# Where the reciprocal square roots of all row norms are computed: eight VectorE instructions, or two or three on GpSimd

## The chip, the cores and the metric

The kernel runs on one core of a Trainium2 chip. The metric is the device time of one execution in microseconds (us). A core has five engines that run their own instruction streams and wait for each other through semaphores: TensorE (PE in the profile, with PEld for its weight loads), VectorE (DVE), ScalarE (ACT), GpSimd (POOL) and SyncE (SP, which issues the DMAs here).

## The reference, cut to what matters

Two layers of an encoder work on 768 tokens of 1024 features (512 of one request group, "S", and 256 of another, "P"). Layer 0 mixes tokens with a chunked gated unit, layer 1 with long convolutions; both add cross-attention to 256 memory tokens and a gated feed-forward part. Every sub-layer is normalised before and after:

```python
def rms_norm(x, g):
    y = xf * lax.rsqrt(jnp.mean(xf * xf, axis=-1, keepdims=True) + NORM_EPS)
    return y * g
def layer_norm(x, g, b):
    return (xf - mu) * lax.rsqrt(var + LN_EPS) * g + b
...
    hn = rms_norm(x, p['norm_mix_pre'][i])
    ... out = jnp.concatenate([mix, att], axis=-1) @ p['w_out'][i]
    x = x + rms_norm(out, p['norm_mix_post'][i])
    hn = rms_norm(x, p['norm_ffn_pre'][i])
    f = conv_ffn(hn, ...)
    x = x + rms_norm(f, p['norm_ffn_post'][i])
```

## The kernel before, in words

Tokens are handled in six row tiles of 128 (t = 0 to 3 are S, 4 and 5 are P). Every float32 operand of a large product is split into two parts ("hi" and "lo"), and a product is three matmuls; ACT writes hi, DVE writes lo (`split`). Rows become feature-major operands (`hT`, tiles hTS and hTP) by eight transposes on PE for each row tile (tiles `tps`), split by ACT and DVE.

`rstd_of` turns one column of 128 sums of squares into 128 reciprocal square roots. It is called 62 times: 24 times in `pre_norm` (tile names rstd, rstdm, rstdq: six at the start, and six behind the first output projection, the first down projection and the second output projection), 24 times in `out_proj`'s `half1` (rpost: six in each of four projections, which here are called out0, down0, out1 and down1), 8 times in `kv` (mr) and 6 times in `norm_v` (lnr). Behind a projection one row tile passes through this chain: the last matmul of its bank (rp), ACT's Square with a sum, rpost, two DVE instructions that add the residual (xr), for all but the last projection ACT's Square of the new x, rstd, DVE's scaling (y, or hn at the start), eight transposes on PE, the split. At the end of the program the two xr halves go out by DMA.

The order in which an engine takes its instructions is not written by hand. `Order` records what the kernel states and then runs a list schedule: each engine takes, among the instructions that it takes for ready, the one of the lowest rank; rank is the place in the stated order plus an offset from the table BIAS, and readiness comes from the durations in `cost` and the delays in LAT. So the numbers in `cost`, and the count of instructions stated ahead, set the order on all engines. Engines run their streams in that order. The attention's score matmuls (tiles `sc`) use 64 of the 128 rows of the array, two heads on the two halves; the other large products use 128 rows.

Of the kernel before, what the change touches and what calls it, by code (L numbers as in the profile page):

```python
# [30 lines left out]
# Buffers that the kinds of tiles may hold at once.  # L31
ROLES = {'xr': ('x', 3), 'y': ('y', 4), 'x0': ('x', 3), 'mem': ('mem', 2), 'mn': ('mem', 2), 'praw': ('pr', 2), 'hn': ('y', 4)}
T4, WR, WS, M8, M4 = 7, 2, 4, 14, 13
# How far in stated order the schedule may run ahead of its oldest instruction left, and by how many places the
# instructions of a part of the kernel (by kind) stand later than stated when an engine chooses.
# [52 lines left out]
def rstd_constants(n):  # L88
    """Newton's step and the third-order step on r multiply its limit by factors of their own; so the estimate aims
    at -(z / m) ** 0.5, the first step at (a / m) ** 0.5 and the second at (n / m) ** 0.5."""  # L90
    k1 = (3.0 * math.sqrt(n) / 8.0) ** 0.2
    k0 = (k1 / 2.0) ** (1.0 / 3.0)
    return k0 * k0, k1 * k1, float(0x5F3759DF + math.log2(k0) * 2 ** 23 - 2 ** 31)

class Order:
    """Takes down instructions as the kernel states them and hands them to Tile in the order of a list schedule:
    whenever an engine is free it takes the first stated instruction whose operands and buffers are there."""  # L100
# [17 lines left out]
    @contextmanager  # L118
    def of(self, part=None, load=None):
        """What is stated inside belongs to this part of the kernel; loads are the weights' way in."""  # L120
        keep = self.part, self.load
        self.part, self.load = part or self.part, self.load if load is None else load
        yield
        self.part, self.load = keep
# [8 lines left out]
    def tile(self, pool, shape, dt, tag, bufs, name, kind=None, cap=0):  # L133
        """A tile takes one of its tag's buffers, and one of the cap that its kind may hold."""
        t = pool.tile(list(shape), dt, tag=tag, name=name, bufs=bufs)
        self.tiles[t.tensor.name] = dict(res=[(tag, bufs)] + ([(kind, cap)] if kind else []), ops=[])
        return t

# [60 lines left out]
    @staticmethod  # L199
    def cost(eng, method, kw, args, outs, ins):  # L200
        n = max(int(np.prod([c for s, c in x.ap[1:]])) for x in outs)
        psum = any(x.space == bass.MemoryType.PSUM for x in ins)
        if eng == "tensor":
            if method == "transpose":
                return 110
            if kw["rhs"].dtype == F32R:
                return n / 2.4 if n >= 256 else 229
            return 20 + 4 * n / 2.4
        if eng == "scalar":
            c = (52 if psum else 95) + 0.833 * n  # L210
            return c + (190 if isinstance(kw.get("bias"), bass.AP) or isinstance(kw.get("scale"), bass.AP) else 0) + \
                (90 if "accum_out" in kw else 0)
        if eng == "vector":
            if method in ("tensor_scalar", "tensor_copy") and not psum:
                return 68 + 0.522 * n
            if method == "tensor_reduce" or method == "bn_stats":
                n = max(int(np.prod([c for s, c in x.ap[1:]])) for x in ins)
            return (130 if method == "scalar_tensor_tensor" else 69) + 1.042 * n
        if eng == "gpsimd":
            return 148 + 2.105 * n  # L220
        return 450

# [1 line left out]
    def schedule(self):  # L224
# [42 lines left out]
        def allowed(i):  # L267
            """Buffers for the tiles that start at i; the instructions before it must still fit in stated order."""
            at = ready_t[i]
            for name in first.get(i, ()):  # L270
                for tag, b in self.tiles[name]["res"]:
                    j = pos[name, tag]
                    if not free[tag]:
                        return None
                    at = max(at, min(free[tag]))
                    s, k = seq[tag], nxt[tag]
                    while k < len(s) and s[k][0] < oldest:
                        k += 1
                    nxt[tag] = k
                    if k < j:  # L280
                        later = sum(1 for x in ahead[tag] if x >= k)
                        live = sum(1 for x in s[max(0, k - 4 * b):k] if left[x[2]])
                        if live + later + 1 > b:
                            return None
                        for q in range(k, j):
                            if q in ahead[tag]:
                                later -= 1
                            elif left[s[q][2]] and serial[tag][q] + later + 1 > b:
                                return None
            return at  # L290
# [90 lines left out]
class FM:  # L381
    """Feature-major hi/lo pair: k-tiles of 128 features, S tokens and P tokens in tiles of their own."""
# [29 lines left out]
class Pairs:  # L412
    """Feature-major hi/lo pair in tiles of two k-tiles each."""
# [18 lines left out]
class Prog:  # L432
# [47 lines left out]
    def presplit(self):  # L480
        """Layer 1's mixer weights split while the matrix products of layer 0's feed-forward part hold the time."""
# [28 lines left out]
    def rstd_of(self, ss, n, eps, name, add=None):  # L510
        """(ss / n + eps) ** -0.5 (ss + add for ss when there is one), from an estimate out of the exponent bits by
        one step of second and one of third order; the steps' factors are folded into the estimate."""
        v = self.nc.vector
        m = self.small([128, 1], name + "m")
        r = self.small([128, 1], name)
        q = self.small([128, 1], name + "q")
        if add is None:
            v.tensor_scalar(out=m, in0=ss, scalar1=n * eps, scalar2=None, op0=ALU.add)
        else:
            v.scalar_tensor_tensor(out=m, in0=ss, scalar=n * eps, in1=add, op0=ALU.add, op1=ALU.add)  # L520
        z, a, magic = rstd_constants(n)
        v.tensor_scalar(out=r.bitcast(I32), in0=m.bitcast(I32), scalar1=-0.5, scalar2=magic, op0=ALU.mult, op1=ALU.add)
        v.scalar_tensor_tensor(out=q, in0=r, scalar=m, in1=r, op0=ALU.mult, op1=ALU.mult)
        v.scalar_tensor_tensor(out=r, in0=q, scalar=-3.0 * z, in1=r, op0=ALU.add, op1=ALU.mult)
        v.scalar_tensor_tensor(out=q, in0=r, scalar=m, in1=r, op0=ALU.mult, op1=ALU.mult)
        v.scalar_tensor_tensor(out=q, in0=q, scalar=-10.0 / 3.0 * a, in1=q, op0=ALU.add, op1=ALU.mult)
        v.scalar_tensor_tensor(out=r, in0=q, scalar=5.0 * a * a, in1=r, op0=ALU.add, op1=ALU.mult)
        return r

# [24 lines left out]
    def rows_proj(self, nk, lhs, load, tail, done, gen=None, order=None, pre=()):  # L554
        """lhs(c) -> f(h, kk, t): [128, 128] of k-tile 2c + kk; done(t, bank); pre: chunks of W loaded before."""
# [336 lines left out]
    def dft_load(self, name):  # L892
        """S: [hi | lo][mat, 128 cols], P: [hi | lo][mat, 128 cols]."""
# [9 lines left out]
    def fwd_S(self, prod, out, two_sided=False):  # L903
        """prod(o, m, r, cs): matrix m of the residue-major [cos | sin] list times part cs of the tokens 4 r' + r;
        out: [128, 2, 1024] = [Z0 | Z3], [Z2 | Z1], each [c | s].
        For a two-sided filter -t has another residue than t when t is odd, so the turned spectra of the odd
        residues take the filter's sum and difference with cos and sin the other way round."""
# [29 lines left out]
    def fwd_P(self, prod, out):  # L937
        """prod as for S, of the tokens 2 r' + r; out: [128, 1024] = [Z | Z~], each [c | s]."""
# [95 lines left out]
    def times_k(self, y, kk, n):  # L1034
        """y *= kk as complex numbers c - i s; both [128, n, 2, 256]; n spectra; kk is used up."""
# [9 lines left out]
    def conv_S(self, prod, o, th):  # L1045
        """-> [128, 4, 2, 256]: the four residues' [c | s] spectra before the inverse."""
# [22 lines left out]
    def conv_P(self, prod, o, th):  # L1069
        """-> [128, 2, 2, 256]: [sum | difference][c | s]."""  # L1070
# [13 lines left out]
    def mixer_b(self, hT, kvo):  # L1084
# [12 lines left out]
        def spectra(zt):  # L1097
            """Products of the forward matrices with S's, P's tokens as rows by residue."""
# [10 lines left out]
        def rows_of(th, part):  # L1109
            """Tokens as rows, by residue: four of S, two of P."""  # L1110
# [86 lines left out]
    def run(self):  # L1197
# [3 lines left out]
        make_identity(self.tc.nc, self.ident)  # L1201
        hT, pre = FM(self, "hT"), []
# [120 lines left out]
```

## Time and profile before

| | |
|---|---|
| time, median of 3 runs | 1844.01 us (1843.69 to 1844.19) |
| span of the profiled execution | 1843.3 us, 0.7 us under that median |
| PE busy | 1818.3 us, 99% of the span |
| DVE busy | 1040.1 us, 56% |
| ACT busy | 644.6 us, 35% |
| POOL busy | 0.7 us, 6 instructions |
| DMA | 210 MB moved, 114 GB/s in the mean |

The profile gives one execution. Busy time counts an engine's instructions; a wait is idle time of an engine, put down to what ended it. The chain of work is followed back from the last instruction, at each step to what released it; its pieces on PE run from the start of one matmul to that of the next, so they show how fast matmuls follow each other, while the duration of one matmul also holds the time in which it overlaps the next.

### The profile page before, as it was taken

Reading aid. Unit: us, or ns where it says so; the run is one execution under the profiler, and the core shown is the slowest. Engines: PE = TensorE matmul, PEld = TensorE weight load, DVE = VectorE, ACT = ScalarE, POOL = GpSimd, SP = SyncE. Lnnn points to the kernel's source line nnn. Section 1 sums busy time; section 2 is a strip of 40 time slices with the busy share of each in tenths; the row PEclk is TensorE's granted clock in tenths of the full one; section 3 lists DMA queues with packets and bytes.
Section 4 is the critical chain, followed back from the end, with each engine's and each line's share of the span. In section 5 each row is a group of like instructions: output and inputs, shape, how many; then the busy total and the mean of one; then the engine's idle time right before and its main releaser. Section 6 shows DMA issues by size and latency. Waiting matters only on the chain. (4 is left out here: it accounts for less than half of the span.)

```text
span 1843.3 us, 23844 instructions
## 1 busy us (share of the span) xinstructions
PE 1818.3 (99%) x9732; PEld 1535.0 (83%) x9732; DVE 1040.1 (56%) x1886; ACT 644.6 (35%) x1018; POOL 0.7 (0%) x6
## 2 busy tenths in 40 slices
PE   7999999999999999999999999999999999999998
PEld 6878878788888888888898888777888888888886
DVE  7456576646554665574968876777433233444523
ACT  5373343323322334463521224344222222333510
POOL 0000000000000000000000000000000000000000
PEclk9999999999999999999999999999999999999999
DMA  8022233222232223788743240223411121213112
GB/s 302 27 85 93 67 115 126 64 97 86 69 124 100 81 70 135 270 323 343 271 175 108 110 149 12 103 69 135 162 58 50 54 69 40 64 36 102 61 54 103
DMA packets 54444, 210.23 MB, mean 114 GB/s; under 512 B 6099, under 2 KB 6303, under 8 KB 49216
## 3 DMA queue, kind: packets, MB, share of 16 engines
q1 hardware_dynamic: 54336, 208.72, 32.3%
q8 instruction: 76, 1.25, 0.3%
q14 instruction: 32, 0.26, 0.0%
HBM read 165.70 MB, written 42.99 MB: 113 GB/s over the span
## 5 line engine op out<-in xcount | busy, mean ns | idle before, releaser
L370 PE MATMUL fmp<-hTP,ws 128*128 128x256 f32 x2640 | 714.9, 286 | 0.0
L370 PEld LDWEIGHTS fmp<-hTP,ws 128*128 128x128 f32 x2640 | 491.8, 190 | 9.7 <-issue 3.7
L370 PE MATMUL fmb<-hTS,ws 128*128 128x512 f32 x1320 | 482.5, 401 | 0.0
L370 PE MATMUL fma<-hTS,ws 128*128 128x512 f32 x1320 | 474.4, 399 | 0.7 <-ACT hTS L370 0.6
L370 PEld LDWEIGHTS fmb<-hTS,ws 128*128 128x128 f32 x1320 | 248.0, 188 | 63.1 <-issue 6.2
L370 PEld LDWEIGHTS fma<-hTS,ws 128*128 128x128 f32 x1320 | 248.1, 188 | 59.5 <-ACT hTS L370 1.4
L370 PE MATMUL rp<-ws,xsS 128*128 128x512 f32 x1056 | 278.1, 390 | 0.0
L370 DVE TENSOR_TENSOR ws<-wr,ws 128x1024 fp32r<-128x1024 f32 x166 | 202.2, 1221 | 86.6 <-ACT ws L370 86.5
L370 PEld LDWEIGHTS rp<-ws,xsS 128*128 128x128 f32 x1056 | 198.0, 188 | 41.4
L370 ACT ACTIVATE ws<-wr 128x1024 fp32r<-128x1024 f32 x166 | 173.6, 1051 | 81.7 <-PE rp L370 48.8
L370 DVE SCALAR_TENSOR_TENSOR gate<-fma,cv,gate 128x511 f32<-128x511 f32 x88 | 65.7, 746 | 188.2 <-ACT gate L370 186.9
L370 PE MATMUL rp<-ws,xsP 128*128 128x512 f32 x528 | 157.8, 392 | 0.0
L370 PEld LDWEIGHTS rp<-ws,xsP 128*128 128x128 f32 x528 | 98.8, 188 | 20.8
L370 PE MATMUL rp<-ws,mxS 128*128 128x512 f32 x384 | 105.3, 410 | 0.3 <-ACT mxS L370 0.3
L370 ACT ACTIVATE gate<-fma,cv 128x512 f32<-128x512 f32 x44 | 34.0, 773 | 197.5 <-PE fma L370 195.7
L370 PE MATMUL rp<-ws,hTS 128*128 128x512 f32 x288 | 85.6, 407 | 2.1 <-ACT hTS L370 2.1
L370 PEld LDWEIGHTS rp<-ws,mxS 128*128 128x128 f32 x384 | 72.0, 190 | 17.0 <-ACT mxS L370 0.7
L370 DVE SCALAR_TENSOR_TENSOR gate<-fmp,cv,gate 128x255 f32<-128x255 f32 x88 | 42.1, 478 | 77.0 <-ACT gate L370 76.5
L370 DVE TENSOR_TENSOR xsS<-hS,xsS 128x1024 fp32r<-128x1024 f32 x44 | 53.4, 1223 | 55.1 <-ACT xsS L370 55.1
L370 ACT ACTIVATE gate<-fmp,cv 128x256 f32<-128x256 f32 x44 | 24.8, 564 | 167.2 <-PE fmp L370 167.2
L370 ACT ACTIVATE xsS<-hS 128x1024 fp32r<-128x1024 f32 x44 | 46.1, 1056 | 69.1 <-PE rp L370 49.6
L370 PEld LDWEIGHTS rp<-ws,hTS 128*128 128x128 f32 x288 | 54.4, 193 | 14.1 <-ACT hTS L370 2.5
(234 smaller groups left out, 2084.7 us busy)
## 6 DMA issues: line engine op xcount, KB each, us to landing
wr<-w_up SPq DMA_DIRECT2D x88, 512.0 KB, 3.7
wr<-w_down SPq DMA_DIRECT2D x44, 512.0 KB, 4.7
wsp<-pw SPq DMA_DIRECT2D x20, 1024.0 KB, 10.8
ws<-wsp SPq DMA_DIRECT2D x20, 1024.0 KB, 6.6
xs<-xr SPq DMA_DIRECT2D x18, 512.0 KB
praw<-bw SPq DMA_DIRECT2D x18, 512.0 KB, 7.5
xr<-xs SPq DMA_DIRECT2D x18, 512.0 KB, 4.8
wr<-w_out SPq DMA_DIRECT2D x16, 512.0 KB, 3.6
```

The costliest lines, as they stand in the source:

```text
L370: getattr(getattr(self.real, eng), method)(*args, **kw)
```

## The change

`rstd_of` is stated on GpSimd: a multiply and add (sum / n + eps), and a power with the exponent from a column of -0.5; where two sums are added, one more add ahead of these. The column is filled once at the start. The eight VectorE instructions, their constants and the third small tile go. In the schedule's `cost`, a float32r matmul of 256 or more columns gets 13.5 more, and a GpSimd instruction 180 in place of 148. BIAS is the same table. (The diff's other lines are comments.)

```diff
-                return n / 2.4 if n >= 256 else 229
+                return 13.5 + n / 2.4 if n >= 256 else 229
...
-            return 148 + 2.105 * n
+            return 180 + 2.105 * n
...
     def rstd_of(self, ss, n, eps, name, add=None):
-        v = self.nc.vector
+        g = self.nc.gpsimd
         m = self.small([128, 1], name + "m")
         r = self.small([128, 1], name)
-        q = self.small([128, 1], name + "q")
-        if add is None:
-            v.tensor_scalar(out=m, in0=ss, scalar1=n * eps, scalar2=None, op0=ALU.add)
-        else:
-            v.scalar_tensor_tensor(out=m, in0=ss, scalar=n * eps, in1=add, op0=ALU.add, op1=ALU.add)
-        z, a, magic = rstd_constants(n)
-        v.tensor_scalar(out=r.bitcast(I32), in0=m.bitcast(I32), scalar1=-0.5, scalar2=magic, op0=ALU.mult, op1=ALU.add)
-        v.scalar_tensor_tensor(out=q, in0=r, scalar=m, in1=r, op0=ALU.mult, op1=ALU.mult)
-        v.scalar_tensor_tensor(out=r, in0=q, scalar=-3.0 * z, in1=r, op0=ALU.add, op1=ALU.mult)
-        v.scalar_tensor_tensor(out=q, in0=r, scalar=m, in1=r, op0=ALU.mult, op1=ALU.mult)
-        v.scalar_tensor_tensor(out=q, in0=q, scalar=-10.0 / 3.0 * a, in1=q, op0=ALU.add, op1=ALU.mult)
-        v.scalar_tensor_tensor(out=r, in0=q, scalar=5.0 * a * a, in1=r, op0=ALU.add, op1=ALU.mult)
+        if add is not None:
+            g.tensor_tensor(out=m, in0=ss, in1=add, op=ALU.add)
+            ss = m
+        g.tensor_scalar(out=m, in0=ss, scalar1=1.0 / n, scalar2=eps, op0=ALU.mult, op1=ALU.add)
+        g.tensor_tensor(out=r, in0=m, in1=self.half, op=ALU.pow)
         return r
...
+        self.half = self.cst.tile([128, 1], F32, name="half")
+        self.tc.nc.gpsimd.memset(self.half, -0.5)
```

The schedule moves instructions on every engine. Three places follow.

PE in layer 0's attention, at the last scores of the P tokens: before, the scores of the two heads (sc_300, sc_301) stand in a row.

```order
L370 MATMUL sc_300<-kT,qP 128x256
L370 MATMUL sc_301<-kT,qP 128x256
L370 MATMUL sc_300<-kT,qP 128x256
L370 MATMUL sc_301<-kT,qP 128x256
L370 MATMUL sc_300<-kT,qP 128x256
L370 MATMUL sc_301<-kT,qP 128x256
L370 MATMUL rp_328<-ws,hTS_85 128x512
```

The same place after the change, with the heads' tiles called sc_292 and sc_293.

```order
L360 MATMUL sc_292<-kT,qP 128x256
L360 MATMUL rp_320<-ws,hTS_87 128x512
L360 MATMUL sc_292<-kT,qP 128x256
L360 MATMUL rp_325<-ws,hTS_87 128x512
L360 MATMUL sc_292<-kT,qP 128x256
L360 MATMUL rp_325<-ws,hTS_89 128x512
L360 MATMUL rp_330<-ws,hTS_83 128x512
L360 MATMUL sc_293<-kT,qP 128x256
L360 MATMUL rp_325<-ws,hTS_87 128x512
L360 MATMUL sc_293<-kT,qP 128x256
```

Scores now stand one by one between matmuls of 128 rows. In the whole program 47 of the 144 score matmuls stood alone between others before, and 58 do after; in layer 0 alone it is 11 and 24.

PE behind the second output projection (out1), at the transposes of row tile 1 (tile y_1615) before:

```order
L370 MATMUL tps_1624<-ident_76,y_1615 128x128
L370 MATMUL rp5_1665<-ws_1597,mxP2_1508 128x512
L370 MATMUL tps_1624<-ident_76,y_1615 128x128
L370 MATMUL rp5_1665<-ws_1597,mxP2_1508 128x512
L370 MATMUL tps_1624<-ident_76,y_1615 128x128
L370 MATMUL rp5_1665<-ws_1599,mxP3_1404 128x512
L370 MATMUL tps_1624<-ident_76,y_1615 128x128
```

And after (row tiles 0 and 1 are y_1560 and y_1571):

```order
L360 MATMUL tps_1567<-ident_76,y_1560 128x128
L360 MATMUL tps_1568<-ident_76,y_1560 128x128
L360 MATMUL tps_1578<-ident_76,y_1571 128x128
L360 MATMUL tps_1568<-ident_76,y_1560 128x128
L360 MATMUL tps_1578<-ident_76,y_1571 128x128
L360 MATMUL tps_1568<-ident_76,y_1560 128x128
L360 MATMUL tps_1578<-ident_76,y_1571 128x128
```

Before, 47 matmuls of the projection (rp) stand between the first and the last of the 32 transposes of S; after, two, and the projection's matmuls stand ahead.

DVE at the end of the program, row tiles 4 and 5, before (a piece of it; rpostm, rpost and rpostq belong to `rstd_of`):

```order
L370 SCALAR_TENSOR_TENSOR rpostq_1999<-rpostq_1999 128x1
L370 SCALAR_TENSOR_TENSOR rpostq_2005<-rpost_2004,rpostm_2003 128x1
L370 SCALAR_TENSOR_TENSOR rpost_1998<-rpostq_1999,rpost_1998 128x1
L370 SCALAR_TENSOR_TENSOR rpostq_2005<-rpostq_2005 128x1
L370 SCALAR_TENSOR_TENSOR xr_1994<-fP_1867,rpost_1998,xr_1994 128x512
L370 SCALAR_TENSOR_TENSOR xr_1994<-y_1995,rpost_1998,xr_1994 128x512
L370 SCALAR_TENSOR_TENSOR rpost_2004<-rpostq_2005,rpost_2004 128x1
L370 SCALAR_TENSOR_TENSOR xr_2000<-fP_1867,rpost_2004,xr_2000 128x512
L370 SCALAR_TENSOR_TENSOR xr_2000<-y_2001,rpost_2004,xr_2000 128x512
```

And after:

```order
L360 TENSOR_TENSOR y_1937<-rp4_1874,gpost_1815 128x512
L360 TENSOR_TENSOR y_1942<-rp5_1875,gpost_1815 128x512
L360 SCALAR_TENSOR_TENSOR xr_1936<-fP_1813,rpost_1940,xr_1936 128x512
L360 SCALAR_TENSOR_TENSOR xr_1936<-y_1937,rpost_1940,xr_1936 128x512
L360 SCALAR_TENSOR_TENSOR xr_1941<-fP_1813,rpost_1945,xr_1941 128x512
L360 SCALAR_TENSOR_TENSOR xr_1941<-y_1942,rpost_1945,xr_1941 128x512
```

The six GpSimd instructions of the two row tiles (two adds, two multiplies with add, two powers) stand on POOL. On PE the last matmuls of banks rp4 and rp5 alternate to the end after the change; before, the last four were rp5's alone.

## Rows read from the trace of the kernel before

**Rows 1.** The page: the span, and the busy time of each engine with its share of the span.
```profile
span 1843.3 us, 23844 instructions
PE 1818.3 (99%) x9732; PEld 1535.0 (83%) x9732; DVE 1040.1 (56%) x1886; ACT 644.6 (35%) x1018; POOL 0.7 (0%) x6
```

**Rows 2.** The waits of PE: engine, tile and what ended the wait; us in total, times, longest.
```profile
PE tps L370 <- DVE hn L370: 10.0, 1, 10.0
PE rp L370 <- ACT hTS L370: 2.1, 1, 2.1
PE tps L370 <- DVE y L370: 1.6, 1, 1.6
PE rp L370 <- DVE pS L370: 1.2, 1, 1.2
PE fma L370 <- ACT hTS L370: 0.6, 1, 0.6
```

**Rows 3.** The chain of work in stretches of the two attentions, and its last long stretch: start, us, what. A piece runs to the next one's start.
```profile
1125.43 1.14 PE sc L370 x16
...
1158.22 0.31 PE sc L370
1158.53 0.31 PE fmp L370
...
1220.68 0.31 PE sc L370
1221.00 0.43 PE rp L370
...
1661.27 173.30 PE rp L370 x765
```

**Rows 4.** The end in order of time: row tiles 4 and 5.
```profile
1833.88 0.60 ACT L370 ACTIVATE y<-rp 128x512 f32<-128x512 f32 x1 [8.65 <-issue]
1834.37 0.19 ACT L370 ACTIVATION_READ_ACCUMULATOR y<-rp 128x1 f32 x1
1834.60 0.69 DVE L370 TENSOR_TENSOR y<-rp,gpost 128x512 f32<-128x512 f32 x1 [4.52 <-ACT y L370]
1834.78 0.60 ACT L370 ACTIVATE y<-rp 128x512 f32<-128x512 f32 x1 [0.22 <-ACT y L370]
1835.50 0.69 DVE L370 TENSOR_TENSOR y<-rp,gpost 128x512 f32<-128x512 f32 x1
...
1837.41 0.75 DVE L370 SCALAR_TENSOR_TENSOR xr<-fP,rpost,xr 128x512 f32<-128x512 f32 x1
1838.08 0.75 DVE L370 SCALAR_TENSOR_TENSOR xr<-y,rpost,xr 128x512 f32<-128x512 f32 x1
...
1839.60 0.74 DVE L370 SCALAR_TENSOR_TENSOR xr<-y,rpost,xr 128x512 f32<-128x512 f32 x1
```

**Rows 5.** Instructions of `rstd_of` in `pre_norm` by group: count, busy us, mean ns of one, idle time before.
```profile
L370 DVE TENSOR_SCALAR rstdm<-ss 128x1 f32<-128x1 f32 x24 | 3.5, 148 | 0.5 <-ACT hn L370 0.3
L370 DVE TENSOR_SCALAR rstd<-rstdm 128x1 int32<-128x1 int32 x24 | 3.5, 148 | 0.1
L370 DVE SCALAR_TENSOR_TENSOR rstdq<-rstd,rstdm 128x1 f32<-128x1 f32 x48 | 9.9, 217 | 0.5
L370 DVE SCALAR_TENSOR_TENSOR rstd<-rstdq,rstd 128x1 f32<-128x1 f32 x48 | 7.1, 156 | 0.6
L370 DVE SCALAR_TENSOR_TENSOR rstdq<-rstdq 128x1 f32<-128x1 f32 x24 | 3.7, 156 | 0.3
```

**Rows 6.** POOL's instructions in order of time: start, duration (us), line, operation, tile, shape.
```profile
0.24 0.10 POOL L1313 MEMSET const-float32-0.0<- 128x1 f32 x1 [0.24 <-issue]
...
1.00 0.29 POOL masks.py:199 TENSOR_SCALAR_AFFINE_SELECT ident<-ident 128x128 f32<-128x128 f32 x1
```

**Rows 7.** The start in order of time, row tile 0: ACT's Square and the read of its sum, the first and last instruction of `rstd_of`, the scaling, the transposes.
```profile
5.61 1.06 ACT L370 ACTIVATE hn<-x 128x1024 f32<-128x1024 f32 x1 [0.23 <-DMA x<-x]
6.57 0.19 ACT L370 ACTIVATION_READ_ACCUMULATOR hn<-x 128x1 f32 x1
6.79 0.15 DVE L370 TENSOR_SCALAR rstdm<-ss 128x1 f32<-128x1 f32 x1 [0.15 <-ACT hn L370]
...
8.07 0.16 DVE L370 SCALAR_TENSOR_TENSOR rstd<-rstdq,rstd 128x1 f32<-128x1 f32 x1
8.55 1.28 DVE L370 SCALAR_TENSOR_TENSOR hn<-x,rstd,gain 128x1024 f32<-128x1024 f32 x1 [0.33 <-DMA gain<-norm_mix_pre]
9.98 1.94 PE L370 MATMUL tps<-ident,hn 128*128 128x128 f32 x8 [9.98 <-DVE hn L370]
```

**Rows 8.** The chain of work: eight transposes in a row.
```profile
1292.95 0.87 PE tps L370 x8
```

**Rows 9.** Behind out1, in order of time: a row tile's scaling, the last transposes of S, the hi and lo parts, the first matmul of the next stage.
```profile
1277.28 1.27 DVE L370 SCALAR_TENSOR_TENSOR y<-xr,rstd,gpre 128x1024 f32<-128x1024 f32 x1
1278.70 1.06 PE L370 MATMUL tps<-ident,y 128*128 128x128 f32 x8 [1.59 <-DVE y L370]
1279.69 1.09 ACT L370 ACTIVATE hTS<-tps 128x512 fp32r<-128x512 f32 x2 [0.55 <-PE tps L370]
1280.34 1.28 DVE L370 TENSOR_TENSOR hTS<-tps,hTS 128x512 fp32r<-128x512 f32 x2
1280.35 0.50 PE L370 MATMUL fma<-hTS,ws 128*128 128x512 f32 x1 [0.58 <-ACT hTS L370]
```

More of the change, by code (lines that the diff above doesn't have):

```diff
@@ L85 @@
 PI_F = float(np.nextafter(np.float32(math.pi), np.float32(0)))
[L88 to L93, printed above, removed]
 class Order:
```

## The prediction, made before the run

> **What bounds the kernel now.** I read the page first. TensorE is busy for 1818.3 of 1843.3 us, VectorE for 1040.1 [rows 1]. So what VectorE is freed of is worth nothing by itself; it counts only where TensorE waits for a norm. The waits of TensorE show where that is: 10.0 us at the start, until the first scaled rows (hn) are there, 2.1 us soon after, and behind out1 1.6 us until a row tile's scaling (y) and 0.6 us until its hi part (hTS) [rows 2]. With 1.2 us for an attention's operand (pS) these are 15.5 us. TensorE's last long stretch ends at 1661.27 + 173.30 = 1834.57 us [rows 3]; in the 8.7 us from there to the end two row tiles are still normalised and stored [rows 4]. Everything else is TensorE at work, and there the order of the matmuls can change the time, which is the second thing to read: the chain of work, whose pieces on TensorE run from one start to the next [rows 3].
>
> **VectorE is relieved.** One `rstd_of` in `pre_norm` costs 3.5 + 3.5 + 9.9 + 7.1 + 3.7 = 27.7 us over 24 calls, 1.15 us each [rows 5]; the other kinds have as many instructions of the same shapes. 62 calls give 72 us off VectorE, 7% of its busy time. It is idle for 44% of the span while TensorE works on, so this is 0 by itself.
>
> **What GpSimd costs.** 148 instructions on one column of 128: 38 calls with two, 24 with three. The trace has no arithmetic on GpSimd. The nearest rows of that engine are a memset of one column, 0.10 us, and an AFFINE_SELECT over 128 columns, 0.29 us [rows 6]. As the far bound I take the longest pass of one instruction in these rows, 1.28 us for 1024 columns on VectorE [rows 7]. I choose 0.25 us an instruction, since the AFFINE_SELECT also reads and writes and one column is less; a power may be dearer, and so 1.28 stays in the range. For the hand-overs the rows give 0.03 us from ScalarE to VectorE (6.76 to 6.79) and 0.15 us from VectorE to TensorE (9.83 to 9.98) [rows 7]; I take 0.2 into GpSimd and 0.1 after that. A call of three is then 0.2 + 3 × 0.25 + 3 × 0.1 = 1.25 us and one of two 0.9 us, against 1.44 us now for `rstd_of` (6.79 to 8.23).
>
> **Start: 0.** ScalarE's sum is read at 6.76, so rstd would be there at 7.66. The scaling waits for the gain's DMA until 8.55 anyway [rows 7]; that hides it up to 0.85 us more, some 0.4 us an instruction. At 1.28 us it is 9.7, which costs 1.2 us. After this ScalarE takes the first hi parts ahead of the third Square, which would start the first product about 1 us earlier, but then TensorE has to wait for the second row tile; I leave ±1.
>
> **Order of the matmuls: +4.4.** In a run, 16 scores take 1.14 us, 0.07 each, because two heads run at the same time on the two halves of the array. Alone between other matmuls a score takes 0.31 us, and its neighbour too is slower: a projection's matmul of 512 columns takes 0.43 us there, against 173.30 / 765 = 0.227 in a run of its own, and the one of 256 columns 0.31 [rows 3]. So one that stands alone costs (0.31 - 0.07) + (0.43 - 0.227) = 0.44 us. There are 58 of them in place of 47. 11 × 0.44 = 4.8; a few of the new neighbours are transposes, whose price beside a score I have no row for, so I take 0.40 and 4.4. Bounds: 0, if the scheduled order lets the stalls of the softmax fall into these slots, and 7, if other switches are dearer too. The other changes of order on TensorE (transposes in runs or alternating with a projection) I count at nothing.
>
> **out0 and out1: -0.5.** After the change the transposes of the four S tiles stand in one run behind the projection. For row tile 3 there are 46 matmuls and 24 transposes between the end of its bank and its first transpose, 46 × 0.227 + 24 × 0.11 = 13.0 us [rows 3, 8]. What it needs: ScalarE's Square 0.8, rpost 1.25, behind row tile 2's two the two xr to 4.2, the Squares of both and a weight's hi part to 6.2, rstd 0.9, a weight's lo part and the scaling: some 9 us. There is room for 4, or up to about 1 us an instruction. But then the run asks its copies at once: 32 transposes take 3.5 us, while ScalarE needs 0.54 us for each of 7 hi parts and VectorE 0.64 us for each of 7 lo parts [rows 9], so the first products wait about 1.4 us, where they waited 2.2 [rows 2]: -0.8. At out0, where TensorE hardly waited, the same run costs +0.3, because the first matmuls of the filter network stand in between.
>
> **down0: +0.4.** Row tile 0 now has 31 matmuls of room (7.0 us) from the end of its bank to its transposes; before it was 53 (12.0 us). It needs 0.2 + 0.7 (Square and sum) + 1.25 + 1.4 (two xr) + 1.3 (Square and sum) + 0.9 + 1.28 + 0.15 = 7.2, with queueing 7.4 us. Each 0.1 us on a GpSimd instruction adds 0.5 here; so with 1.28 us it is +5.
>
> **End: -1.0.** Now the last xr ends at 1840.34. Row tile 4's bank ends three matmuls later than before, so its Square starts at 1833.88 + 0.68 = 1834.56, its sum is read at 1835.24, and rpost is there at 1836.5. VectorE has by then done both y products (0.6 us apart, the second to 1836.6). Four xr at steps of 0.67 end at 1836.6 + 3 × 0.67 + 0.75 = 1839.36 [rows 4]; row tile 5's rpost comes at 1837.6, in time for the third. The store behind is the same. At 1.28 us an instruction, row tile 5's rpost is the late one and the end moves by +4.8; it is even at 0.48 us.
>
> **The sum.** 0 + 4.4 - 0.5 + 0.4 - 1.0 = +3.3, a span of 1846.6. The median of the runs is 0.7 above the profiled span: 1847.3 us, +0.18%. A measurement of this kernel can tell about 0.2% (3.7 us, 1840.3 or 1847.7) from no change.
>
> **A lock between VectorE and GpSimd.** At the end row tile 5's three GpSimd instructions stand beside row tile 4's two xr, each with two operands in SBUF [rows 4]; no row shows both engines at work. If each had to wait for these xr, they would start at 1838.0, rpost would come at 1839.1, and the last xr end at 1840.5: the end is worth +0.2 in place of -1.0, and the sum is +4.5, 1848.5 us. The Trainium skill, SBUF — State Buffer, section "SBUF: two separate sides", speaks for this and so against the change: a VectorE instruction with two SBUF inputs and a GpSimd instruction that reads SBUF share a port pair that one of them holds for its whole length.
>
> **Rivals.** (a) *Slower, by the GpSimd chain.* Its place is the three adds, multiplies and powers between a Square and the xr. From 0.48 us an instruction the end no longer gains, and down0 loses over 1.5 us; at 0.6 us the sum is 4.4 - 0.5 + 2.1 + 0.7 = +6.7 (1850.7), at 1.28 us it is 4.4 + 1.2 + 5 + 4.8 and 3 more at each of out0 and out1, over +20. For it: no row bounds a power from close by, and the lock above works the same way. Against: four of five places have room. Lock included, 0.19.
> (b) *Slower, by a first use.* If the first arithmetic instruction on GpSimd has to fetch its code, each us over the 0.85 us of room at the start delays everything; if it took as long as the engines need from the start to the first sum (6.76 us, [rows 7]), that is +5.9 on top, 1853.2. Against it: the first memset and the AFFINE_SELECT behind it run within 1.3 us of the start [rows 6]. The Trainium skill, GPSIMD Engine Reference, section "Instruction dispatch", gives about 6 us for the first call to a freshly loaded kernel, which would be +5.1 here; no row shows one. Its chance is 0.04.
> (c) *Faster: the relieved VectorE and the new order close waits.* If lone scores cost nothing here because softmax waits fill the gaps, if out1 loses its 2.2 us, the wait for pS its 1.2 us [rows 2], the end 1.0 us and the start 1 us, the sum is -5.4: 1838.6. For it: the wait on y behind out1 ends with VectorE's own work [rows 9]. Against: nothing in the attentions uses `rstd_of`. 0.17.
> (d) *No effect beyond noise because orders even out*, sum within ±1: 0.12.
>
> **The numbers.** The forecast with its terms (1845 to 1849.5) holds 0.48, of which 0.31 lies under 1847.7; with (d) "same" is 0.43. Slower is 0.17 + 0.19 + 0.04 = 0.40, faster 0.17. The range leaves out the far halves of (a) and (c): 1839.5 to 1853.5.
>
> **What would show it.** In the profile after: VectorE busy near 968 us; GpSimd with 148 more instructions, and the mean of one of them decides between 0.25 and 0.5; lone scores at 0.31 with neighbours at 0.43; TensorE's waits on hTS behind out1 1 to 1.5 us; a wait on y at down0; the last xr starting 4.0 us after TensorE's last long stretch, against 5.0 now (1839.60 - 1834.57). I am wrong if GpSimd's instructions take over 0.5 us, if TensorE waits in the attentions for other reasons, or if TensorE's busy time falls.

## The result, and the profile after

The kernel after takes 1865.45 us (median; 1862.95 to 1867.49) against 1844.1: a ratio of 1.0114, interval 1.0098 to 1.0129, so 21 us slower. The forecast of 1847.3 us, between 1839.5 and 1853.5, is wrong: the direction that it leaned to is right, the size is off by 18 us. The page and the clock of the profiled execution:

```profile
span 1860.9 us, 23630 instructions
PE 1827.7 (98%) x9732; PEld 1539.6 (83%) x9732; DVE 992.0 (53%) x1452; ACT 642.8 (35%) x1018; POOL 76.2 (4%) x155
```

Against [rows 1] the span is 17.6 us longer. TensorE is busy for 9.4 us more with the same 9732 matmuls, and idle for 8.2 us more (33.2 against 25.0). The waits of TensorE after, in the columns of [rows 2]:

```profile
PE tps L360 <- DVE hn L360: 9.2, 2, 9.1
PE iv L360 <- DVE pS L360: 4.5, 1, 4.5
PE tps L360 <- DVE hTS L360: 2.8, 2, 1.6
PE tps L360 <- DVE y L360: 2.4, 3, 1.4
PE rp L360 <- DVE x L360: 1.3, 1, 1.3
```

The start is 0.8 us better than in [rows 2], and the wait for y no more than 0.8 us worse. Longer by 3.3 us is the wait that ends with pS, beside layer 1's convolution, where nothing of `rstd_of` runs; new are waits of the transposes for hTS, 1.6 us behind out0 and 1.2 behind out1. That more busy time goes with the same matmuls can mean a dearer order or a slower clock, and the second was nowhere in my sum. These are the windows of 10 us, between 0 and 1830, in which the granted clock is not 1.00 (length; busy us and count of PE, PEld, DVE, ACT, POOL; clock; DMA share, GB/s), after:

```profile
110.00:120.00 10.00, 10.00 (x38) 7.24 (x38) 3.15 (x8) 4.90 (x15) 0.00 (x0) 0.66 0.01 2
280.00:290.00 10.00, 10.00 (x27) 6.17 (x27) 9.19 (x13) 5.92 (x13) 5.93 (x9) 0.66 0.38 136
1180.00:1190.00 10.00, 10.00 (x34) 6.85 (x33) 6.69 (x16) 3.73 (x13) 0.00 (x0) 0.83 0.24 71
1220.00:1230.00 10.00, 6.64 (x33) 6.67 (x34) 9.02 (x17) 0.91 (x2) 0.00 (x0) 0.66 0.17 52
```

and before:

```profile
1160.00:1170.00 10.00, 10.00 (x43) 7.46 (x42) 5.39 (x10) 5.00 (x14) 0.00 (x0) 0.83 0.11 44
1170.00:1180.00 10.00, 10.00 (x39) 7.62 (x39) 5.33 (x13) 4.17 (x11) 0.00 (x0) 0.83 0.34 118
```

The clock has two levels, 2.4 GHz (1.00) and 1.2 GHz (0.50); a window between them holds a stretch of either. The lost shares add up to 0.34 × 30 + 0.17 × 10 = 11.9 us at full speed after and 3.4 before: 8.5 us, nearly all of the 9.4. (About 0.5 us of them falls into the wait for pS.) The order of the matmuls by itself is left with some 1 us in the whole program; ahead of the gate it costs more, as shown below, so elsewhere it must give some back, and where was not measured. This execution also had the highest mean clock of the four, 0.993 against 0.990 in the other three (the kernel before: 0.997). 0.003 of the span is 5.6 us, so by this estimate the clock takes some 14 us of the loss in those three.

**What rstd_of costs on GpSimd.** The groups of POOL (as [rows 5]), and row tile 0 at the start in order of time (as [rows 7]):

```profile
L360 POOL TENSOR_TENSOR rstd<-rstdm,half 128x1 f32<-128x1 f32 x24 | 16.5, 688 | 2.0
L360 POOL TENSOR_TENSOR rpost<-rpostm,half 128x1 f32<-128x1 f32 x24 | 15.9, 664 | 2.0
L360 POOL TENSOR_SCALAR rstdm<-ss 128x1 f32<-128x1 f32 x24 | 13.8, 575 | 39.5 <-ACT y L360 21.2 <-ACT hn L360 13.4 <-DVE xr L360 4.6
L360 POOL TENSOR_SCALAR rpostm<-rpostm 128x1 f32<-128x1 f32 x24 | 7.1, 298 | 2.1
L360 POOL TENSOR_TENSOR rpostm<-s,s 128x1 f32<-128x1 f32 x24 | 5.7, 239 | 1015.7 <-ACT y L360 1015.6
```

```profile
6.86 0.19 POOL L360 TENSOR_SCALAR rstdm<-ss 128x1 f32<-128x1 f32 x1 [5.58 <-ACT hn L360]
7.14 0.56 POOL L360 TENSOR_TENSOR rstd<-rstdm,half 128x1 f32<-128x1 f32 x1
```

Undisturbed, an add or multiply-add takes 0.19 us and a power 0.55; the first ones, from 6.86 on, take no longer than later ones. The means are longer, because some instructions on POOL are stretched while VectorE works with two inputs from SBUF. At down0, POOL, VectorE and TensorE in order of time:

```profile
885.89 1.64 POOL L360 TENSOR_TENSOR rpost<-rpostm,half 128x1 f32<-128x1 f32 x1
...
885.91 1.22 DVE L360 TENSOR_TENSOR wkv<-wr,wkv 128x1024 fp32r<-128x1024 f32 x1
887.57 0.75 DVE L360 SCALAR_TENSOR_TENSOR xr<-fS,rpost,xr 128x512 f32<-128x512 f32 x1 [0.44 <-POOL rpost L360]
...
890.38 0.88 PE L360 MATMUL tps<-ident,y 128*128 128x128 f32 x6 [1.36 <-DVE y L360]
```

The power lies beside the lo part of a weight and takes 1.64 us; rpost comes late, and at the end of its chain TensorE waits 1.36 us. Of the 148, all 37 that are longer than 0.56 us lie beside a VectorE instruction with two SBUF inputs. This is the lock of the prediction. The Trainium skill, SBUF — State Buffer, section "SBUF: two separate sides", gives the lock to whichever starts first; that the two engines exclude each other the trace bears out, but here the power starts 0.02 us earlier by the rows and still waits, and the means of VectorE's weight lo parts (1221 ns) and of its last xr (744 and 745 ns) are those of before.

### The profile page after: what moved, and what is told of

It is laid out like the page before. It is cut to its first block, busy times and chain, and to the rows that moved or that the text cites. A ratio compares the mean times of both kernels' runs of the same rounds, so it can differ in the third digit from the quotient of the medians.

```text
span 1860.9 us, 23630 instructions
## 1 busy us (share of the span) xinstructions
PE 1827.7 (98%) x9732; PEld 1539.6 (83%) x9732; DVE 992.0 (53%) x1452; ACT 642.8 (35%) x1018; POOL 76.2 (4%) x155
## 4 chain that ended last, share of the span: by engine, by line
PE 88%; DVE 6%; issue 2%; ACT 2%; POOL 1%; DMA 1%; SPq 0%; POOLq 0%; DVEq 0%; ACTq 0%
PE rp L360 28%; PE fmp L360 16%; PE fma L360 15%; PE fmb L360 15%; PE dft L360 3%; PE iv L360 2%; PE sc L360 1%; PE h L360 1%; PE kps L360 1%; PE vps L360 1%; PE pv L360 1%; DVE zS L360 1%; DMA wr<-w_up 1%; PE tps L360 1%; PE eps L360 1%
## 5 line engine op out<-in xcount | busy, mean ns | idle before, releaser
L360 PE MATMUL fmp<-hTP,ws 128*128 128x256 f32 x2640 | 725.6, 286 | 0.0
L360 DVE TENSOR_TENSOR ws<-wr,ws 128x1024 fp32r<-128x1024 f32 x166 | 202.2, 1221 | 104.9 <-ACT ws L360 104.7
L360 PE MATMUL rp<-ws,mxS 128*128 128x512 f32 x384 | 110.1, 410 | 1.3 <-DVE x L360 1.3
L360 DVE TENSOR_TENSOR xsS<-hS,xsS 128x1024 fp32r<-128x1024 f32 x44 | 53.2, 1221 | 40.1 <-ACT xsS L360 40.1
```

What stands on the lines that cost most here:

```text
L360: getattr(getattr(self.real, eng), method)(*args, **kw)
```

## The experiments

The candidates were: **theory 1**, the order of the matmuls; **theory 2**, GpSimd's chain (power and lock), which is rival (a). Medians belong to different series, so runs are compared by the ratio to the kernel before in the same series; 0.1% is 1.8 us. (`rstd_of` had seven VectorE instructions, not eight as written above; the 1.15 us were summed over all of them.)

**Instructions and order apart.** The schedule is made with one version of `rstd_of`; when the instructions are issued, the other version takes its place:

```diff
             for i in order:
+                if i in self.swap:
+                    for eng, method, kw in self.swap[i]:
+                        getattr(getattr(self.real, eng), method)(**kw)
+                    continue
```

> The order of every engine's instructions is that of the kernel before (1844.1 us), and only the instructions of rstd_of are other ones: two or three on GpSimd in place of seven on VectorE. Theory 1 (the new order is what costs the 21 us: matmuls that stand alone, and TensorE's wait for pS in layer 1): 1844 us, within 3, since nothing on TensorE is moved. Theory 2 (GpSimd's chain is what costs: a power of 0.55 us, and instructions that are stretched while VectorE works with two inputs in SBUF): at least 1852 us, with TensorE waiting for hn at the start and for hTS or y behind out0, down0 and out1.

> The order of every engine's instructions is that of the kernel after (1865.5 us), and only rstd_of is VectorE's estimate and steps again. Theory 1 (order): 1861 to 1866 us, with the same wait of 4.5 us for pS. Theory 2 (GpSimd's chain): 1844.1 + 3.3 for the prices of the matmuls in the new order and about 1 for the shorter room at down0, so 1847 to 1851 us.

Old order with GpSimd: 1842.42 us, ratio 0.9997 (0.9984 to 1.0010). Its page and longest waits:

```profile
PE 1815.9 (99%) x9732; PEld 1533.7 (83%) x9732; DVE 991.2 (54%) x1452; ACT 644.9 (35%) x1018; POOL 80.4 (4%) x155
```

```profile
PE tps L375 <- DVE hn L375: 9.8, 1, 9.8
PE rp L375 <- ACT hTS L375: 2.3, 1, 2.3
PE tps L375 <- DVE y L375: 1.6, 1, 1.6
PE rp L375 <- DVE pS L375: 1.2, 1, 1.2
PE fma L375 <- ACT hTS L375: 0.6, 1, 0.6
```

These are [rows 2] again, within 0.2 us each: in the old order the change of engine does nothing that can be told from 0. New order with VectorE: 1903.29 us, 1.0341 (1.0311 to 1.0370), a miss for both theories. Seven instructions now stand in VectorE's own queue at places that were chosen for another engine's; TensorE waits 8.6 us for y, 7.5 for hTS, 13.6 for hn. So the new order is bad, but this run can't say how bad it is by itself.

**The other lines of the diff.** The two cost lines without, and GpSimd without the two cost lines.

> The kernel before with the two lines of the schedule's cost alone: 13.5 more for a matmul, 180 for a GpSimd instruction; rstd_of stays on VectorE. Theory 1 (order): a new order by itself is worth up to 20 us either way, and this one moves as many rows of TensorE as the whole change does; I expect 1850 or more. Theory 2 (GpSimd's chain): 1844 within 4.

> rstd_of on GpSimd with the cost lines of before, so a third order of the matmuls. Theory 1 (order): anything from 1840 to 1865, since it hangs on the order that comes out; no stretched instructions in the critical places. Theory 2 (GpSimd's chain): 1855 to 1866, as after, since the same instructions stand in the same chains whatever the order.

The cost lines alone take 1866.51 us, 1.0134 (1.0104 to 1.0164), and GpSimd without them 1868.54 us, 1.0135 (1.0118 to 1.0152). With the kernel after these are three new orders, with `rstd_of` on either engine, and all lose 21 to 25 us. The cost lines alone leave `rstd_of` on VectorE, so theory 2 can't be the whole. All three have more scores that stand alone in layer 0's attention (24 after, 24 and 19, against 11), all wait for pS (4.5, 4.4 and 3.1 us, against 1.2), and all have half clocks. But they don't lose in the same places, as the table by stages below has it: GpSimd without the cost lines is only 2.4 us late at the first matmul of layer 0's token mixing (gate), at a clock of 1.00 up to there, and loses most of its time in layer 1, where eight windows between 1170 and 1250 us lie below 1.00 and lose 13.7 us to the clock. What follows is about the order of the kernel after.

**How much room the old order has.** The old order on GpSimd, with the power done twice:

```diff
+        new.append(("gpsimd", "tensor_tensor", dict(out=r, in0=m, in1=self.half, op=ALU.pow)))
         new.append(("gpsimd", "tensor_tensor", dict(out=r, in0=m, in1=self.half, op=ALU.pow)))
```

> The order of the kernel before with rstd_of on GpSimd, and the power done twice: 0.63 us more in each of the 62 chains, the same result. If the old order has room for GpSimd's chain (out0, down0 and out1 end their last rows long before the transposes): within 3 us of 1842.4, with 1 us of it at the end, where the last two row tiles are normalised. If it has none: 0.63 x 2 at each of out0, down0, out1 and the end, and more for a clock that falls in the waits, so 1848 or more.

1843.08 us, 0.9984 (0.9972 to 0.9997): 0.6 us more a chain, 62 times, and no loss. Rival (a) doesn't hold in the old order.

**How much room the new order has.** The kernel after, in its own order, with the chain cut to one instruction:

```diff
-            g.tensor_tensor(out=m, in0=ss, in1=add, op=ALU.add)
-        g.tensor_scalar(out=m, in0=ss, scalar1=1.0 / n, scalar2=eps, op0=ALU.mult, op1=ALU.add)
-        g.tensor_tensor(out=r, in0=m, in1=self.half, op=ALU.pow)
+        g.tensor_scalar(out=r, in0=ss, scalar1=0.0, scalar2=1.0, op0=ALU.mult, op1=ALU.add)
```

> The kernel after, in its order, but rstd_of is one GpSimd instruction that writes the constant 1: the add, the multiply and add, and the power are left out, some 0.8 to 1 us of each chain. Theory 1 (order alone): 1862 or more. Theory 2 (GpSimd's chain): 1848 or less. Both together (the new order leaves less room behind out0, down0 and out1, and the power does not fit into it): 1855 to 1861, with the waits for hTS, y and hn behind projections gone and the wait for pS in layer 1 (4.5 us) unchanged.

1853.88 us, 1.0056 (1.0036 to 1.0077): half of the loss is gone, half stays, and the wait for pS is still 3.0 us. By the traces 4.5 of the 8.8 us that the span is shorter lie at out0, whose wait for hTS and half clock are gone, and 2.5 in layer 1. So neither theory is the whole; in the new order the chain has too little room.

**Where the loss lies.** The places of all instructions in both orders are known; a kernel takes one order up to a mark, and what is left in the other:

```diff
         order = self.schedule()
+        n = next(p for p, i in enumerate(one) if i in self.marks[CUT])
+        done = set(one[:n])
+        order = one[:n] + [i for i in two if i not in done]
```

> rstd_of on GpSimd. Instructions are issued in the order of the kernel after until its first matmul of layer 0's token mixing (gate), what is left then in the order of the kernel before. If the loss is local, made where matmuls, waits and clock differ, this has what the kernel after has lost up to there: its first gate starts at 191.9 us, with the order of before on GpSimd at 183.6, so 1842.4 + 8 = 1850. If the loss is that of whole chains, or lies in layer 1 alone: 1842 to 1845.

> As the run before, with the order of the kernel after until the first product of the filter network (h3), so with attention, token mixing and out0 of layer 0. Local loss: first h at 360.9 against 349.0, so 1842.4 + 12 = 1854. Otherwise within 2 us of the run before.

> As the two runs before, with the order of the kernel after until the first memory weight of layer 1 (wkv). Local loss: nothing is lost within layer 0's feed-forward part (its dft products come 12.7 us later, as late as at its start), so 1855, and the remaining 10 us of the kernel after belong to down0, layer 1's mixer and out1.

> rstd_of on GpSimd; the order of the kernel before until the first matmul of token mixing (gate), what is left then in the order of the kernel after: the counterpart of the run that changes over the other way at the same place. If the losses add: 1865.5 less the 10 of the part ahead of the gate, so 1854 to 1857. If they don't, since out0 and layer 1 lose by what the start leaves them: below 1848 or above 1860.

> rstd_of on GpSimd, the order of the kernel before until the first memory weight of layer 1 (wkv), what is left then in the order of the kernel after. With the order of before until the gate the time was 1850.9, 8.5 above the old order throughout, and 1.4 of that lay ahead of the end of layer 0's filters. If the rest is layer 1's own (TensorE runs out of matmuls while VectorE works through the convolution: the wait for pS of 4.5 us, a half clock behind it): 1848 to 1851. If it comes from what is done early or late in layer 0: 1842 to 1845.

| order | time, us | ratio (interval) |
|---|---|---|
| new until gate, then old | 1855.28 | 1.0050 (1.0031 to 1.0070) |
| new until the filters | 1853.07 | 1.0043 (1.0027 to 1.0059) |
| new until layer 1 | 1854.37 | 1.0050 (1.0028 to 1.0071) |
| old until gate, then new | 1850.94 | 1.0025 (1.0013 to 1.0038) |
| old until layer 1, then new | 1850.09 | 1.0035 (1.0016 to 1.0055) |

What is lost in layer 0 is lost ahead of the gate (8 to 9 us); out0 and the feed-forward part add nothing that these three tell apart. The run with the old order until the gate came out between its two cases: by the ratios it lies 5.2 us above the old order throughout, not the 8.5 that two expectations take from medians of different series. Layer 1 loses 4.6 to 6.5 by itself. The parts make some 14 us, 7 short of 21. One place of the difference can be named: from the first gate to the first product of the filters, the kernel after takes 169.0 us and the one with the old order until the gate, which has the same order there, 164.9. In the kernel after, 28 transposes, a wait and a few small products stand there, and the clock falls:

```profile
278.80 1.25 PE L360 MATMUL tps<-ident,y 128*128 128x128 f32 x8 [1.58 <-DVE hTS L360]
280.00 1.41 PE L360 MATMUL fl<-feat,w 33*64 33x512 f32 x2
281.34 0.79 PE L360 MATMUL fma<-hTS,ws 128*128 128x512 f32 x1
```

In the other run the 28 transposes follow each other without a wait, and its clock is 1.00. That accounts for the 4.1 us; some 3 us of the 7 stay open. Runs of one order differ in such things: the last section has three first gates as an example. The Trainium skill, TensorE: Matmul & The Clock Gate, section "Part 1: The HAM clock gate", says that the gate follows how busy the engine has been and that one kernel meets it differently from run to run; the second agrees. Its first half needs care: ahead of the fall at 110 us TensorE was busy all the time by the profile, as the next rows show.

**Ahead of the gate.** TensorE in the kernel after, in order of time:

```profile
108.56 0.50 PE L360 MATMUL pv<-pS,vS 128*128 128x512 f32 x1
109.00 0.38 PE L360 MATMUL sc<-kT,qS 64*128 64x256 f32 x1
109.31 0.50 PE L360 MATMUL pv<-pS,vS 128*128 128x512 f32 x1
109.74 0.43 PE L360 MATMUL sc<-kT,qS 64*128 64x256 f32 x1
110.10 0.79 PE L360 MATMUL pv<-pS,vS 128*128 128x512 f32 x1
110.83 0.58 PE L360 MATMUL sc<-kT,qS 64*128 64x256 f32 x1
```

For 8 us, from 101.7 on, mostly lone scores alternate with single matmuls of 128 rows, 0.31 and 0.43 us from start to start, as [rows 3] have it; then, at 109.7, with no wait, each takes 1.6 times as long, and at 116.7 full speed is back. All seven traces with 24 lone scores in layer 0 (after, both runs in its whole order, the cost lines alone, the three that are new until the gate) have such a fall that begins between 109 and 118 us; none of the other ten, with 2 to 19 of them, has a fall ahead of 270 us. The test moves the twelve scores of two heads and two row tiles (g) into one run, behind the last thing that they need (place p), and nothing else:

```diff
         order = self.schedule()
+        pos = {i: p for p, i in enumerate(order)}
+        for g in groups.values():
+            p = max([pos[g[1]]] + [pos[d] for i in g for d in self.ops[i][4] | self.ops[i][7] if d not in g])
+            move.setdefault(order[p], []).extend(i for i in g if pos[i] > p)
```

> The kernel after with one change: the scores of layer 0's attention alone are moved together in the same way (lone scores 58 to 36). If the loss ahead of the gate is that of lone scores and of the half clock that follows them: 22 x 0.40 = 8.8 us for the switches and 2 to 4 for the clock, so 1852 to 1855, and a granted clock of 1.00 from 100 to 120 us. If not: 1862 or more.

> rstd_of on GpSimd in the order of the kernel before, and on TensorE the twelve scores of two heads and two row tiles are moved forward to stand in one run, right behind the last thing that they need: scores that stand alone go from 47 to 5, nothing else is moved. If a lone score costs 0.4 us (its own 0.31 against 0.07, and its slower neighbour): 42 x 0.40 = 17 us less, so 1826. If the lone scores fill the gaps in which TensorE would wait for the softmax: 1838 to 1844, and new waits for e, pS or pP.

> The kernel before, rstd_of on VectorE, with the scores moved together as in the run of 1830.4 us that has rstd_of on GpSimd. If the two changes are independent and GpSimd is worth nothing by itself: 1830 to 1833, the same within 2 us. If the moved scores give their gain only with a relieved VectorE: 1838 or more.

In the kernel after, with layer 0's scores alone: 1848.37 us, 1.0008 (0.9998 to 1.0019). By the ratios 19 to 20 us of the 21 are gone, more than the 11 to 13 that I had worked out. TensorE's time for the scores between 80 and 160 us (window and columns as above), in the kernel after, with the scores together, and in the old order on GpSimd:

```profile
80.00:160.00 80.00, 14.53 (x72) 8.20 (x72) 8.04 (x12) 12.37 (x48) 0.96 0.25 83
```

```profile
80.00:160.00 80.00, 7.70 (x72) 5.94 (x72) 7.97 (x12) 12.29 (x48) 1.00 0.27 92
```

```profile
80.00:160.00 80.00, 9.84 (x72) 6.23 (x72) 7.78 (x12) 12.43 (x48) 1.00 0.27 90
```

The clock is 1.00 throughout this window, and the first gate starts at 180.8 us instead of 191.9. Out0 now takes 165.4 us in place of 169.0, though nothing was moved there: its half clock is gone too, and its wait for hTS is 0.5 us in place of 1.6; why the wait is shorter was not traced. The trace's span is 15.3 us shorter; by my estimate 22 × 0.41 = 9.0 of them are the switches (the 0.41 is worked out in the section on the prediction), 3.4 the clock ahead of the gate and 3.6 out0. The test does more than undo the change: 2 lone scores are left in layer 0, where the kernel before has 11, and these nine are worth some 3.7 us. So lone scores and clock account for some 16 of the 21 us, and the rest is not taken away by this test: the wait for pS, 4.5 us, is still there. The other two runs put the scores of both layers together (47 alone become 5) in the old order: 1830.36 us with `rstd_of` on GpSimd, 0.9908 (0.9893 to 0.9923), and 1831.08 with it on VectorE, 0.9931 (0.9916 to 0.9946). Both beat either kernel; the medians are 0.7 us apart and the intervals overlap, so the engine of `rstd_of` can't be told in them. Between the traces of the old order on GpSimd the span shrinks by 11.0 us (1839.4 to 1828.4) where I had worked out 17: 4.8 us come back as waits (pS 3.0 in place of 1.2, e 1.5, zS 0.8, T 0.7).

**Behind the gate.** The old order until the gate, the new one behind it, with the chain cut to one instruction as above.

> The run with the order of before until the gate and the order of after behind it (1850.9), but rstd_of is one GpSimd instruction that writes the constant 1 (add, multiply and power left out). It tells how much of the 8.5 us behind the gate is GpSimd's chain in the new order. If it is the chain: 1843 to 1845. If it is the order: 1849 to 1851. By the waits of that run for y, hTS and hn behind projections, some 3 us are the chain's: 1847 to 1848.

1845.60 us, 1.0007 (0.9996 to 1.0017), against 1.0025 with the chain. The 2.4 us of waits for y are gone; by its trace 2.0 of the 5.1 us of span come from ahead of the gate, 0.5 from out0, 2.1 from down0 to up1, 0.5 from the end. So some 3 us behind the gate are the chain's in this order, as worked out from the waits. What stays is the wait for pS:

```profile
PE tps L479 <- DVE hn L479: 9.0, 1, 9.0
PE iv L479 <- DVE pS L479: 4.5, 1, 4.5
```

In the kernel after, TensorE and VectorE around it:

```profile
1216.03 2.88 PE L360 MATMUL rp<-ws,mxP 128*128 128x512 f32 x12
1223.36 0.98 PE L360 MATMUL iv<-dfti,A 128*128 128x128 f32 x3 [4.46 <-DVE pS L360]
...
1219.59 1.23 DVE L360 TENSOR_TENSOR U<-zS 128x1024 f32<-128x1024 f32 x1
1220.73 1.22 DVE L360 TENSOR_TENSOR V<-zS 128x1024 f32<-128x1024 f32 x1
1221.94 0.67 DVE L360 TENSOR_TENSOR A<-U 128x512 f32<-128x512 f32 x1
1222.53 1.28 DVE L360 TENSOR_TENSOR pS<-eps,pS 128x512 fp32r<-128x512 f32 x2
```

VectorE works without a gap through the convolution (zS, U, V, A) with pS behind it, and TensorE has run out of out1's matmuls. Behind the wait it goes on at half clock:

```profile
1224.00:1228.00 4.00, 4.00 (x21) 4.00 (x21) 3.93 (x9) 0.00 (x0) 0.00 (x0) 0.50 0.03 4
```

By these rows 3.3 us of new wait and some 3 of clock stand here. That the wait makes the clock fall is read from their sequence; no run took the wait alone away. The other traces agree with it. In ten of them the wait for pS behind 1170 us lasts 3.0 to 4.5 us, and in each a half clock of 3.4 or 6.8 us begins within the wait or at most 1.0 us behind it; in the six where it lasts 1.2 us none begins within 10 us. Likewise at out0: the four traces whose transposes wait there for hTS, 1.58 to 3.9 us, have a half clock that begins in the wait or at most 3 us behind it, and no other trace has one there.

**The trace by stages.** Starts of four matmuls and the span, us:

| kernel | first gate | first filter product | sixth dft group | last up1 | span |
|---|---|---|---|---|---|
| before | 184.5 | 349.9 | 678.3 | 1642.7 | 1843.3 |
| old order, GpSimd | 183.6 | 349.0 | 677.4 | 1640.3 | 1839.4 |
| after | 191.9 | 360.9 | 690.1 | 1658.9 | 1860.9 |
| after, chain of one | 190.6 | 355.1 | 684.3 | 1650.6 | 1852.1 |
| cost lines alone | 192.2 | 358.2 | 687.1 | 1663.4 | 1866.9 |
| GpSimd, costs of before | 186.9 | 356.3 | 684.5 | 1663.6 | 1865.7 |
| after, layer 0's scores together | 180.8 | 346.2 | 675.4 | 1643.6 | 1845.6 |
| old until gate, then new | 184.6 | 349.5 | 678.8 | 1646.9 | 1848.9 |
| the same, no power | 182.6 | 347.0 | 676.3 | 1642.3 | 1843.8 |

After minus before: +7.4 to the gate, +3.6 at out0, +0.8 in the feed-forward part, +4.4 from there through layer 1's mixer and up1, +1.4 at the end, in this one execution. The two other new orders lose 12 to 15 us between the sixth dft group and the last up1, where the kernel after loses 4.4; why was not tested.

## Why the prediction was wrong, step by step

- **VectorE relieved, worth 0: right.** 48 us went off VectorE's busy time, not 72: 26 of the 74 us that its instructions of `rstd_of` lasted had lain over a neighbour's. The old order on GpSimd shows what that is worth: nothing within 0.15%.
- **GpSimd's price: the sum right, its parts wrong.** 0.25 us an instruction was 0.19 for the adds and 0.55 for the power, over the 0.5 from which I would have been wrong by my own words. A chain of two was taken as 0.9 us; at the start rstd is there at 7.70 us, and 7.66 was forecast. The lock stretches single powers to 1.64 us. With the old order even another 0.6 us a chain is hidden.
- **Start 0: right. End -1.0: right in sign.** The first transposes start 0.9 us earlier, within the ±1; the end behind TensorE's last matmul is 0.6 us shorter.
- **Order of the matmuls, +4.4: this step failed.** The price of a lone score held: up to the gate 13 more of them cost the scores, pv and fmp 7.0 us from start to start in a run whose clock fell only briefly (new until the filters, 1.7 us lost), so 5.3 / 13 = 0.41 each. The net count of 11 was right too. What failed is that I priced them at full clock and set the upper bound at 7 without it: 13 more stand in layer 0's attention and 2 fewer in layer 1, and in layer 0 the clock falls to 1.2 GHz after 8 us of them, with no wait ahead of it. The runs showed some 16 us in place of 4.4: with the scores there together 19 to 20 of the 21 us go, 3.7 of them by lone scores that the kernel before has too. 5.3 of the 16 are switches; in the traces the clock ahead of the gate is another 3.4 and out0 3.6; the last 4 are the difference between the medians and these two traces, and what they are stays open. In [rows 3] every matmul runs at full speed, so no row there could carry this price; but from 1095 to 1240 us, with layer 1's attention in it, the clock before was 0.98, and I hadn't asked why.
- **Other changes of order, counted at nothing: failed too.** I asked what waits for a norm, since the change is about norms. But the new order also left TensorE short of matmuls beside VectorE's convolution: 4.5 us for pS where I had read 1.2.
- **Out0, out1 and down0, -0.1 together: too low.** down0's wait is 1.36 us for the first row tile, through the stretched power; I had 0.4. Out0's transposes in one run were put at +0.3, and cost 1.6 us of wait and a half clock behind it in this execution. Behind out1 TensorE waits 3.3 us for y and hTS, where it waited 2.2 and I had 1.4.
- **Rivals.** (a), GpSimd's chain alone, is refuted in the old order; in the new one cutting the chain gives back half of the loss. (b), a first use, is refuted at 6.86 us. (c) and (d) did not happen. None of them named the clock.

## What to carry to other kernels

Where a planner sets the order from costs and offsets, even a small edit is a change of order: hold the order fixed and swap the instructions alone to learn what an instruction is worth (here nothing), then look at what the new order does. On a TensorE that is busy for 99%, look for alternations of half-array and full-array matmuls and price them twice: the switch (0.4 us here), and the half clock that followed a long series of them here (3.4 us each time that it lasted 7). Keeping such matmuls in runs was worth 0.7 to 0.9%, where the change of engine by itself was worth nothing.

## What the runs showed of the hardware that I had not expected

- The clock fell to 1.2 GHz while TensorE's records were without a gap, after 8 us of lone 64-row and single 128-row matmuls. It came back during a series of alternating rp and fmp, both with 128 rows, 7 us later. With the scores in runs it stayed at 1.00.
- The same instructions in the same order lose more or less to the clock from one execution to the next: between 110 and 150 us the profiles of the three kernels that are new until the gate lost 10.2, 1.7 and 1.7 us, and their first gates start at 198.2, 190.7 and 189.9 us.
- A power on one column of GpSimd takes 0.55 us, an add or multiply-add 0.19; beside a VectorE instruction with two SBUF inputs it lasts until after that one has ended (in the kernel after, by 0.05 us for a multiply-add and 0.41 for a power), at most 2.37 us (a multiply-add at out0 in the old order on GpSimd). VectorE's instructions got no longer.
